# Gate and up products over both token streams at once in a four-layer transformer trunk

## Chip, cores and metric

The kernel runs as one launch on one core of a Trainium2 chip. The metric is the device time of that launch in microseconds (us); lower is better. The engines are named as in the profile: PE multiplies matrices, PEld is its load of the stationary operand, DVE, ACT and POOL are the vector, scalar and general engines, and SP issues the DMAs.

## What is computed

Two streams of 256 tokens by 1024 features pass through four layers: the latent tokens `x` (stream l) and the context tokens `ctx` (stream c). They share all weights. Each layer is

```python
h  = rmsnorm(x,   g[0]) * (1.0 + sc1)  + sh1
hc = rmsnorm(ctx, g[0]) * (1.0 + csc1) + csh1
y, yc = mixer(h, hc)          # layers 0 and 3: differential attention, 1: neighbourhood, 2: windowed
x = x + gt1 * rmsnorm(y, g[1])
h = rmsnorm(x, g[2]) * (1.0 + sc2) + sh2
x = x + gt2 * rmsnorm((silu(h @ w1) * (h @ w3)) @ w2, g[3])
# the same for ctx, but not after the attention of the last layer
```

Context tokens attend only to context tokens, latent tokens to both. The shifts, scales and gates come from `silu(c) @ ada_w[i] + ada_b[i]` (and from `c_ctx` for the context). The hidden width of the feed-forward part is 2816, which is 22 blocks of 128 columns for gate and 22 for up.

## The kernel before

**Arithmetic.** Every matrix product is done in three: each fp32 factor is split into a rounded part (hi) and the rest (lo), and `mm3` (L486 to L489) issues hi·hi, hi·lo and lo·hi into one sum. Weights come in units of 512 KB. `load_weight` (L494) loads a unit into `wr` by one DMA, ACT rounds it into `wh`, and DVE subtracts to get `wl` (L501). There are 3 tiles `wr`, and 5 each of `wh` and `wl` (RING), so at most five units are on the chip in split form.

**Products.** `feature_major` (L785) takes one unit of 128 columns of the weights for one stream: the weights are the stationary operand, h transposed is the moving one, 256 columns wide (the tokens of one stream). A unit is 8 blocks of features by 3 products, 24 matmuls, in two operations of 12. It serves q, k, gate and up. `token_major` (L794, for w2) and `block_unit_product` (L1119, for v and o) have the tokens as the stationary operand and the weights as the moving one, 512 columns wide. For gate and up, one PSUM bank per stream and pair holds gate in columns 0 to 255 and up in 256 to 511; then ACT takes the silu and DVE multiplies (L1270).

**Tiles of h.** h transposed lies in tiles of 128 features by 256 tokens: `hh` (hi) and `hl` (lo), 8 of each per stream, in four pools.

**Order.** Nothing runs in the order of the code. `Plan` collects operations with an engine, an estimated duration, a priority and their dependencies, schedules them four times over with a model of the engines, keeps the order of the schedule with the shortest modelled time, and emits each engine's instructions in that fixed order. The durations of PE in it are constants: 12 × 0.109 us for twelve matmuls of 256 columns, 6 × 0.216 us for six of 512; those of ACT and DVE come from `t_act` and `t_dve` (for n elements, `t_dve` gives 0.07 + 0.00104 × n us). The products of a stream keep their order (`chain`, L470). Stream l starts 21.5 us behind stream c in priority (LEAD), so that one stream's products run while the other one is in its norms.

**Beside it.** The shifts, scales and gates of the next layer are computed during gate and up: DVE multiplies and adds rows of `ada_w` (L605, L608), PE sums and transposes them (L615, L649), at a low priority.

**Stages.** By the lines that run, gate and up of layers 0, 1 and 2 lie at about 291 to 555, 933 to 1195 and 1515 to 1778 us from the start of the span, each followed by w2 for 120 us. Layer 3 has only stream l from its queries on; its gate and up run from 2093 to 2220 us.

Of the kernel before, what the change touches and what calls it, by code (L numbers as in the profile page):

```python
# [17 lines left out]
P = 128  # L18
# [38 lines left out]
X_LATE = False  # L57
LATE = 5
# [10 lines left out]
class Buf:  # L69
    """A piece of on-chip memory; `kind` names the slots that it may take, at the time when it is scheduled."""  # L70
# [8 lines left out]

class Bag(dict):  # L80
    """A set that keeps its order."""
# [21 lines left out]
class Plan:  # L103
    """Orders the operations of all engines: earliest first, then by priority, within the slots that there are."""
# [34 lines left out]
    def run(self):  # L139
        """Schedules again and again, each time by the latest starts that the schedule before would allow."""  # L140
# [178 lines left out]
def trunk(ctx: ExitStack, tc: tile.TileContext, a: dict, out: bass.AP, layers=tuple(range(DEPTH)), info=None):  # L319
# [47 lines left out]
    def tick(dt):  # L367
        clock[now[0]] += dt
# [8 lines left out]
    def act(o, i, func, dur, reads, writes, p=None, **kw):  # L377
        """o, i, and the bias/scale/accum_out in kw: functions that return the access, or constants."""
# [54 lines left out]
    def late_consts():  # L433
        """What the first attention needs."""
# [36 lines left out]
    def pe(dur, fn, reads, writes, p=None, also=(), unit=False):  # L471
# [4 lines left out]
        if unit:  # L476
            if now[0] in chain:
                o.after.add(chain[now[0]])
            chain[now[0]] = o
        anchor[now[0]] = o  # L480
        trail[now[0]].append(o)
        if p is None:
            tick(dur)
        return o
# [31 lines left out]
    def ada_load(raw, src, early=False):  # L516
        """Loads of these weights stay in order, and go no further ahead than the tiles and the stream allow."""
# [9 lines left out]
    def ada_first(i, r):  # L527
        """Shift and scale of 256 features, for the first layer: they come piece by piece."""
# [29 lines left out]
    def ada_groups(groups):  # L558
        """Yields after each slice of work; a group: layer, third, halves of it, parts (of 8) of the sum for the vector engine."""
# [5 lines left out]
    def spread(tag, i, m, what):  # L565
        """Vectors of both streams -> DRAM, for reading them on every partition. what: (name, column, function of (out, s))."""
# [24 lines left out]
    def ada_group(i, g, m, us, kd):  # L591
        """Columns g*2048 + u*1024 + j*256 + c stand in row 32j (latent) and 32j+1 (context), column u*256 + c."""
# [80 lines left out]

    def split(s, src_fn, src, hb, lb):
# [4 lines left out]
    def prenorm(s, i, which):  # L679
        """x -> h^T in parts, feature-major, one pair of buffers per 128 features."""  # L680
# [24 lines left out]
        for kp in range(4):  # L705
# [26 lines left out]
    def modulate_first(s, raw, r):  # L732
        """Two times 128 features of h^T in parts, for the first layer."""
# [6 lines left out]
        for kk in range(2):  # L740
            k = 2 * r + kk
            v, hb, lb = Buf("f1"), Buf("hh" + s), Buf("hl" + s)
# [7 lines left out]
    def on_all(s, i, nm):  # L750
        """A vector of 1024 features on every partition, in two halves."""
# [11 lines left out]
    def postnorm(s, i, which, y, final=False):  # L763
        """x += gate * rmsnorm(y): y is [token tile][half] in PSUM."""
# [20 lines left out]
    def feature_major(s, w, H, bank, c0, also=()):  # L785
        """bank[:, c0:c0+T] = (unit of weights)^T h^T."""
        wh, wl, h3, l3 = w
        for half in range(2):
# [3 lines left out]
            pe(12 * 0.109, go, [wh, wl] + [b for k in range(4 * half, 4 * half + 4) for b in H[k]], [bank], also=also, unit=True)  # L792

    def token_major(s, w, hb, lb, y, first, last):  # L794
        wh, wl, h3, l3 = w
        for t in range(2):
# [4 lines left out]
            pe(6 * 0.216, go, [wh, wl, hb, lb], [y[t][0], y[t][1]] if not first else [y[0][0], y[0][1], y[1][0], y[1][1]] if t == 0 else [y[t][0], y[t][1]], unit=True)  # L801

    def rope(bank):
        sw, t1 = Buf("f1"), Buf("f1")
        src = lambda: bank.ap[:, 0:T]
# [9 lines left out]
    def split_q(qs, buf, src):  # L815
        """Two heads of q^T * scale, each as parts stacked over the partitions."""
# [7 lines left out]
    def split_k(buf, src, place):  # L824
        """Two heads of k^T: per head parts (hi, lo), each on both halves of the partitions."""
# [36 lines left out]
    def flip(s, e, pt, qts):  # L862
        """e[q, keys] -> parts of its transpose in pt[pair of key tiles][keys, key tile, q]."""
# [18 lines left out]
    def pt_tiles(s, nkt):  # L882
        """P^T as parts (hi, lo) for each pair of key tiles: [keys, key tile, q]."""
# [5 lines left out]
    def att_a(S, s, j, L):  # L889
# [36 lines left out]
        pe(0.327 * nkt, pv, [b for q in pt for b in q] + [v[0] for v in vals], [(b, 0)])  # L926
# [11 lines left out]
    def att_bc(S, s, j, L):  # L938
# [11 lines left out]
        for m in range(2):  # L950
# [53 lines left out]
            pe(0.218 * nkt, go, [b for q in pt for b in q] + [v[0] for v in vals], [pv])  # L1004
# [7 lines left out]
    def bias_tile(h, qt):  # L1012
        """Relative-position bias and window of the neighbours; nothing is added for the context's keys, which come first."""
# [83 lines left out]
    def make_V(s, kind, y, half=0):  # L1097
        """The values as parts, token-major: V[t] -> access [tokens, head, (hi, lo), dims]."""
# [22 lines left out]
    def block_unit_product(s, w, H, y, h, pr):  # L1121
        """y[t][h] += tokens x (256 features) x (512 columns)."""
# [5 lines left out]
        for t in range(2):  # L1128
            def go(t=t):
# [4 lines left out]
            pe(6 * 0.216, go, [wh, wl] + [b[0::2] if isinstance(b, tuple) else b for kk in range(2) for b in H[2 * pr + kk]],  # L1134
               [y[0][h], y[1][h]] if pr == 0 and t == 0 else [y[t][h]], unit=True)

    def run_unit(s, L, unit, w):
# [4 lines left out]
        if nm == "v":  # L1142
# [3 lines left out]
            if kind == "C":  # L1146
# [4 lines left out]
                for t in range(2):  # L1151
# [7 lines left out]
                    pe(12 * 0.109, go, [wh, wl] + [b for kk in range(4) for b in H[4 * n + kk]], [S.y[t][0]], unit=True)  # L1159
# [12 lines left out]
        elif nm in "qk":  # L1172
            if nm == "q" and n == 0:
                S.o = Buf("oo" + s)
            b = Buf("bk" + s, cap=("proj" + s, CAP_P))
            place, also = None, []
            if nm == "q":
                also = [Buf("r2", cap=("qs", CAP_Q))]
            elif kind != "C":
                also = [Buf("r2", cap=("ks" + s, CAP_K[s])) for _ in range(2)]  # L1180
                place = lambda m: (also[m], lambda: also[m].ap)
            else:
                ra = S.ra

                def place(m):
                    c0 = 1024 + (2 * n + m) * 512
                    return ra, lambda: ra.ap[:, c0:c0 + 512].rearrange("p (l t) -> p l t", l=2)
            feature_major(s, w, S.H, b, 0, also)
            if s == "l" and kind != "B":
                buf, src = rope(b)  # L1190
            else:
                buf, src = b, lambda: b.ap[:, 0:T]
            if nm == "q":
                S.qs = also[0]
                split_q(S.qs, buf, src)
            elif kind == "C":
                for m, kt in enumerate(split_k(buf, src, place)):
                    S.KS[2 * n + m] = kt
            else:
                S.ks = split_k(buf, src, place)  # L1200
                if s == "c":
                    ctx_keys[n] = S.ks
            if (nm == "k" or kind == "C" and nm == "q") and not (kind == "C" and nm == "k") and not (last and s == "c"):
                boost[0] = BOOST[kind]
                (att_a if kind == "A" else att_bc)(S, s, n, L)
                boost[0] = 0.0
                if n == KD - 1:
                    S.gate = trail[s][-GATE[kind]]
        elif nm == "o":
# [7 lines left out]
            if h == 0:  # L1217
                for k in (2 * pr, 2 * pr + 1):
# [5 lines left out]
                    else:  # L1224
                        hb, lb = Buf("hh" + s), Buf("hl" + s)
# [15 lines left out]
        elif nm == "w2":  # L1241
# [3 lines left out]
            hb, lb = Buf("hh" + s), Buf("hl" + s)  # L1245
# [182 lines left out]
```

## Time and profile before

| | |
|---|---|
| device time, median of 3 runs | 2291.74 us |
| lowest and highest | 2291.06 and 2293.13 us |
| span of the profiled execution | 2287.6 us |
| median above that span | 4.1 us |
| PE busy | 2234.2 us, 98% of the span |
| PEld busy | 2064.8 us, 90% |
| DVE busy | 1646.0 us, 72% |
| ACT busy | 1072.1 us, 47% |
| granted clock of TensorE, mean | 0.997 |

The span goes from the first to the last instruction of the profiled execution. Its own total beside the span is not listed, so the 4.1 us are the distance of the median to that span. Matmuls overlap in the pipeline, so the busy time of PE does not tell how densely they are issued; the distance of their starts does.

### The profile page before, as it was taken

Reading aid. Unit: us, or ns where it says so; the run is one execution under the profiler, and the core shown is the slowest. Engines: PE = TensorE matmul, PEld = TensorE weight load, DVE = VectorE, ACT = ScalarE, POOL = GpSimd, SP = SyncE. Lnnn points to the kernel's source line nnn. Section 1 sums busy time; section 2 is a strip of 40 time slices with the busy share of each in tenths; the row PEclk is TensorE's granted clock in tenths of the full one; section 3 lists DMA queues with packets and bytes.
Section 4 is the critical chain, followed back from the end, with each engine's and each line's share of the span. In section 5 each row is a group of like instructions: output and inputs, shape, how many; then the busy total and the mean of one; then the engine's idle time right before and its main releaser. Section 6 shows DMA issues by size and latency. Waiting matters only on the chain.

```text
span 2287.6 us, 41639 instructions
## 1 busy us (share of the span) xinstructions
PE 2234.2 (98%) x16116; PEld 2064.8 (90%) x16116; DVE 1646.0 (72%) x3145; ACT 1072.1 (47%) x2305; POOL 219.7 (10%) x300
## 2 busy tenths in 40 slices
PE   7999999999999999999999999999999999998998
PEld 5899899999888998999998898899999888997997
DVE  5988699886354888978673389998777426896454
ACT  5478642223344776522233368852222325686443
POOL 0111100000010221100000033010000001320000
PEclk9999999999999999999999999999999999999999
DMA  9644366654233443665542330255555333444654
GB/s 305 207 124 125 93 225 204 217 191 150 86 130 98 111 101 107 195 197 185 189 157 92 129 93 20 75 166 189 192 181 176 102 111 111 125 116 145 184 188 139
DMA packets 369302, 339.30 MB, mean 148 GB/s; under 512 B 33120, under 2 KB 282960, under 8 KB 369104
## 3 DMA queue, kind: packets, MB, share of 16 engines
q1 hardware_dynamic: 369104, 336.63, 46.6%
q8 instruction: 127, 2.08, 0.4%
q14 instruction: 71, 0.58, 0.1%
HBM read 321.77 MB, written 1.17 MB: 141 GB/s over the span
## 4 chain that ended last, share of the span: by engine, by line
PE 84%; DVE 7%; ACT 4%; issue 2%; POOL 1%; DMA 1%; SPq 0%; DVEq 0%; ACTq 0%; POOLq 0%
PE bkl L487 14%; PE bkl L488 14%; PE bkl L489 14%; PE bkc L487 11%; PE bkc L489 11%; PE bkc L488 11%; ACT f L388 2%; DVE wl L501 1%; PE bkl L871 1%; PE bkc L615 1%; DVE col L859 1%; ACT r L388 1%; DVE r L879 1%; PE bkl L851 1%; PE bkl L713 1%
## 5 line engine op out<-in xcount | busy, mean ns | idle before, releaser
L501 DVE TENSOR_TENSOR wl<-wr,wh 128x1024 fp32r<-128x1024 f32 x380 | 473.3, 1247 | 380.5 <-ACT wh L388 379.3
L388 ACT ACTIVATE wh<-wr 128x1024 fp32r<-128x1024 f32 x380 | 402.3, 1060 | 697.6 <-PE bkl L488 379.8
L487 PE MATMUL bkl<-hhl,wh 128*128 128x256 f32 x1872 | 532.7, 285 | 0.0
L489 PE MATMUL bkl<-hhl,wl 128*128 128x256 f32 x1872 | 529.2, 283 | 0.0
L488 PE MATMUL bkl<-hll,wh 128*128 128x256 f32 x1872 | 528.4, 282 | 0.0
L487 PE MATMUL bkc<-hhc,wh 128*128 128x256 f32 x1456 | 413.6, 284 | 0.1
L489 PE MATMUL bkc<-hhc,wl 128*128 128x256 f32 x1456 | 411.2, 282 | 0.0
L488 PE MATMUL bkc<-hlc,wh 128*128 128x256 f32 x1456 | 410.9, 282 | 0.1
L608 DVE SCALAR_TENSOR_TENSOR f<-f,cs,f 128x512 f32<-128x512 f32 x556 | 384.7, 745 | 18.3 <-DMA f<-in_ada_w 18.2
L487 PEld LDWEIGHTS bkl<-hhl,wh 128*128 128x128 f32 x1872 | 357.3, 191 | 3.6 <-issue 3.3
L489 PEld LDWEIGHTS bkl<-hhl,wl 128*128 128x128 f32 x1872 | 357.6, 191 | 0.0
L488 PEld LDWEIGHTS bkl<-hll,wh 128*128 128x128 f32 x1872 | 357.4, 191 | 0.2
L487 PEld LDWEIGHTS bkc<-hhc,wh 128*128 128x128 f32 x1456 | 277.1, 190 | 3.5 <-issue 2.5
L488 PEld LDWEIGHTS bkc<-hlc,wh 128*128 128x128 f32 x1456 | 277.1, 190 | 0.8 <-DVE hlc L727 0.3
L489 PEld LDWEIGHTS bkc<-hhc,wl 128*128 128x128 f32 x1456 | 277.2, 190 | 0.0
L487 PE MATMUL bkl<-wh,hhl 128*128 128x512 f32 (+1 forms) x560 | 219.5, 392 | 0.0
L489 PE MATMUL bkl<-wh,hll 128*128 128x512 f32 (+1 forms) x560 | 217.0, 388 | 0.0
L488 PE MATMUL bkl<-wl,hhl 128*128 128x512 f32 (+1 forms) x560 | 217.0, 387 | 0.0
L487 PE MATMUL bkc<-wh,hhc 128*128 128x512 f32 (+1 forms) x472 | 186.3, 395 | 0.0
L488 PE MATMUL bkc<-wl,hhc 128*128 128x512 f32 (+1 forms) x472 | 183.0, 388 | 1.8 <-DVE wl L501 1.8
L489 PE MATMUL bkc<-wh,hlc 128*128 128x512 f32 (+1 forms) x472 | 183.0, 388 | 1.0 <-DVE hlc L677 1.0
L669 POOL TENSOR_SCALAR col<-col 128x1 f32<-128x1 f32 x58 | 37.0, 638 | 1505.0 <-ACT j L388 1459.4
(212 smaller groups left out, 3414.2 us busy)
## 6 DMA issues: line engine op xcount, KB each, us to landing
wr<-in_ffn_w SPq DMA_DIRECT2D x264, 512.0 KB, 3.7
f<-in_ada_w SPq DMA_DIRECT2D x384, 256.0 KB, 4.5
wr<-in_a_wqkv SPq DMA_DIRECT2D x48, 512.0 KB, 3.7
f<-gd SPq DMA_DIRECT2D x54, 256.0 KB, 4.9
r<-r SPq DMA_DIRECT2D x96, 128.0 KB, 2.6
wr<-in_b_wqkv SPq DMA_DIRECT2D x24, 512.0 KB, 3.7
wr<-in_a_wo SPq DMA_DIRECT2D x16, 512.0 KB, 3.7
wr<-in_c_wqkv SPq DMA_DIRECT2D x12, 512.0 KB, 3.7
```

The source lines that it names most:

```text
L388: nc.scalar.activation(o(), i(), func, **k)
L487: nc.tensor.matmul(o, lh, rh, start=first, stop=False)
L488: nc.tensor.matmul(o, lh, rl, start=False, stop=False)
L489: nc.tensor.matmul(o, ll, rh, start=False, stop=last)
L501: dve(lambda: nc.vector.tensor_tensor(l.ap, raw.ap, f32(h.ap[:]), ALU.subtract), t_dve(1024), [raw, h], [l], p)
L608: dve(lambda b=b, raw=raw, c=c: nc.vector.scalar_tensor_tensor(b.ap, raw.ap, c(), b.ap, ALU.mult, ALU.add), t_dve(512, extra=0.06), [raw, ...
L615: nc.tensor.matmul(acc.ap[32 * j:32 * j + 32, u * 256:(u + 1) * 256], lhs, tiles[j // 2].ap[:, (j % 2) * 256:(j % 2 + 1) * 256], start=fir ...
L669: op("pool", 0.25, lambda: nc.gpsimd.tensor_scalar(r.ap[:, 1:2], ss.ap[:, 0:1], ss.ap[:, 1:2], D * EPS, ALU.add, ALU.add), [ss], [r])
L713: nc.tensor.transpose(tp.ap[:, c0:c0 + P], xn[t, k // 4].ap[:, (k % 4) * P:(k % 4 + 1) * P], ident.ap)
L851: nc.tensor.matmul(o, q, kt()[:, 0, :], start=True, stop=False)
L859: dve(lambda: nc.vector.tensor_reduce(nm.ap[:, 0:n], b.ap[:].rearrange("p (i k) -> p i k", i=n), AX.X, ALU.max, negate=True), t_dve(512), ...
L871: nc.tensor.transpose(tp.ap[:, to * P:(to + 1) * P], e.ap[:, c * P:(c + 1) * P], ident.ap)
```

## The change

Gate and up of layers 0 to 2, from the third pair on (`ALONE = 2`), are done by one operation for both streams: the moving operand is h of context and latent side by side, 512 columns. For this, h lies in 8 tiles `both_h[k]` of shape 128 × (hi, lo) × (c, l) × 256. `View` hands out the part of such a tile as if it came from a pool, and `pair(s, k)` names the part of block k, so that a buffer now has a fixed place for each k where before any of 8 would do. Gate gets a whole bank and up another. One silu covers both streams, and two multiplications follow, one for each. The first two pairs, and all of layer 3, are done as before, stream by stream. The products of q and k go into a new function `head_unit`, which is called for one stream (`QK_BOTH` is False), with the same operations as before.

All constants for the durations of matmuls in the planner change, those of ACT, DVE, POOL and DMA do not.

```diff
+ALONE = 2
+QK_BOTH = False
...
-        pool("hh" + s, KD, ("hh" + s, (P, T), R32))
-        pool("hl" + s, KD, ("hl" + s, (P, T), R32))
...
+    both_h = []
+    for k in range(KD):
+        both_h.append(res.tile([P, 2, 2, T], R32, name=f"h{k}", tag=f"h{k}"))
+        for n, s in enumerate("cl"):
+            for m, x in enumerate("hl"):
+                pool(f"h{x}{s}{k}", 1, (f"h{x}{s}{k}", (P, T), R32), mem=View(both_h[k][:, m, n, :]))
...
+    def pe(dur, fn, reads, writes, p=None, also=(), unit=False, streams=None):
...
+        for s in streams or (now[0],):
+            if unit:
+                if s in chain:
+                    o.after.add(chain[s])
+                chain[s] = o
+            anchor[s] = o
+            trail[s].append(o)
+            if p is None:
+                clock[s] += dur
...
+    def pair(s, k):
+
+        return Buf(f"hh{s}{k}"), Buf(f"hl{s}{k}")
...
-            pe(12 * 0.109, go, [wh, wl] + [b for k in range(4 * half, 4 * half + 4) for b in H[k]], [bank], also=also, unit=True)
+            pe(12 * 0.120, go, [wh, wl] + [b for k in range(4 * half, 4 * half + 4) for b in H[k]], [bank], also=also, unit=True)
+
+    def feature_major_both(w, H, bank, also=()):
+
+        wh, wl, h3, l3 = w
+        for half in range(2):
+            def go(half=half):
+                for k in range(4 * half, 4 * half + 4):
+                    hi, lo = (both_h[k][:, m].rearrange("p s t -> p (s t)") for m in range(2))
+                    mm3(bank.ap[:], h3()[:, k, :], l3()[:, k, :], hi, lo, k == 0, k == KD - 1)
+            reads = [wh, wl] + [b for h in H for k in range(4 * half, 4 * half + 4) for b in h[k]]
+            pe(12 * 0.227, go, reads, [bank], also=also, unit=True, streams="cl")
...
-        pe(0.436, go, [qs] + [k[0] for k in keys], [b], also=[e])
+        pe(0.472, go, [qs] + [k[0] for k in keys], [b], also=[e])
...
-        pe(0.327 * nkt, pv, [b for q in pt for b in q] + [v[0] for v in vals], [(b, 0)])
+        pe(0.36 * nkt, pv, [b for q in pt for b in q] + [v[0] for v in vals], [(b, 0)])
...
-            pe(0.218 * nkt, go, [b for q in pt for b in q] + [v[0] for v in vals], [pv])
+            pe(0.24 * nkt, go, [b for q in pt for b in q] + [v[0] for v in vals], [pv])
...
+    def ffn_unit(unit, w):
+
+        nm, n = unit[0], unit[1]
+        bank = Buf("bkl", cap=("gu2", 4))
+        feature_major_both(w, [st[s].H for s in "cl"], bank)
+        if nm == "gate":
+            st["c"].gu2 = bank
+            return
+        gate_bank, sg = st["c"].gu2, Buf("f2")
+        boost[0] = BOOST["F"]
+        act(lambda: sg.ap, lambda: gate_bank.ap, AF.Silu, t_act(512), [gate_bank], [sg])
+        for i, s in enumerate("cl"):
+            g = st[s].g
+            dst, at = (g[0], n) if n < 16 else (g[1], n - 16)
+            dve(lambda i=i, dst=dst, at=at: nc.vector.tensor_tensor(
+                dst.ap[:, at, :], bank.ap[:, i * T:(i + 1) * T], sg.ap[:, i * T:(i + 1) * T], ALU.mult),
+                t_dve(T), [bank, sg], [(dst, at)])
+        boost[0] = 0.0
...
-            hb, lb = Buf("hh" + s), Buf("hl" + s)
+            hb, lb = pair(s, n % KD)
...
+            elif both and unit[0] in ("gate", "up") and unit[1] >= ALONE:
+                now[0] = "c"
+                ffn_unit(unit, w)
```

The six-matmul operations of w2, v and o likewise go from `6 * 0.216` to `6 * 0.227` in the planner, and those of v in layer 2 from `12 * 0.109` to `12 * 0.120`.

## Rows read from the trace of the kernel before

**Rows 1.** The page: share of engines, and the chain by engine.

```profile
PE 2234.2 (98%) x16116; PEld 2064.8 (90%) x16116; DVE 1646.0 (72%) x3145; ACT 1072.1 (47%) x2305; POOL 219.7 (10%) x300
...
PE 84%; DVE 7%; ACT 4%; issue 2%; POOL 1%; DMA 1%; SPq 0%; DVEq 0%; ACTq 0%; POOLq 0%
```

**Rows 2.** Busy time by stage: gate and up, and one w2.

```profile
core 0: us, PE busy (x) PEld busy (x) DVE busy (x) ACT busy (x) POOL busy (x), PEclk, DMA share, GB/s
291.00:555.00 264.00, 263.17 (x2254) 258.84 (x2253) 226.81 (x364) 75.12 (x125) 5.24 (x8) 1.00 0.62 204
555.00:675.00 120.00, 120.00 (x532) 98.73 (x531) 48.09 (x81) 40.55 (x74) 6.22 (x8) 1.00 0.31 106
933.00:1195.00 262.00, 262.00 (x2239) 258.66 (x2238) 208.43 (x330) 75.57 (x127) 5.28 (x8) 1.00 0.58 189
1515.00:1778.00 263.00, 262.05 (x2237) 258.41 (x2236) 207.03 (x337) 75.76 (x127) 6.23 (x8) 1.00 0.57 186
```

**Rows 3.** Forty-microsecond windows of PE alone: gate and up, then w2.

```profile
960.00:1000.00 40.00, 40.00 (x337) 1.00 0.64 205
...
1200.00:1240.00 40.00, 40.00 (x177) 1.00 0.28 97
```

**Rows 4.** Timeline of PE in w2: start, duration, shape.

```profile
559.70 0.40 PE L489 MATMUL bkc<-wh,hlc 128*128 128x512 f32 x1
...
561.10 0.39 PE L489 MATMUL bkc<-wh,hlc 128*128 128x512 f32 x1
561.33 0.39 PE L487 MATMUL bkl<-wh,hhl 128*128 128x512 f32 x1
...
563.37 0.39 PE L487 MATMUL bkl<-wh,hhl 128*128 128x512 f32 x1
```

**Rows 5.** Timeline of PE where stream l comes into gate, layers 0, 1, 2.

```profile
304.20 0.36 PE L487 MATMUL bkl<-hhl,wh 128*128 128x256 f32 x1
...
943.48 1.07 PE L713 MATMUL bkl<-ident,f 128*128 128x128 f32 x8
...
947.68 0.60 PE L713 MATMUL bkl<-ident,f 128*128 128x128 f32 x4
948.04 0.36 PE L487 MATMUL bkl<-hhl,wh 128*128 128x256 f32 x1
...
1528.23 0.36 PE L487 MATMUL bkl<-hhl,wh 128*128 128x256 f32 x1
```

**Rows 6.** Timeline of all engines from up to w2, layer 0.

```profile
552.50 0.28 PE L487 MATMUL bkc<-hhc,wh 128*128 128x256 f32 x1
...
552.98 1.33 ACT L388 ACTIVATE hhl<-gal 128x256 fp32r<-128x256 f32 x4
...
553.46 1.42 DVE L677 TENSOR_TENSOR hll<-gal,hhl 128x256 fp32r<-128x256 f32 x4
...
555.68 0.48 PE L487 MATMUL bkl<-wh,hhl 128*128 128x512 f32 x1
```

**Rows 7.** Groups of DVE and of ACT: count, busy, mean ns, idle before.

```profile
L501 DVE TENSOR_TENSOR wl<-wr,wh 128x1024 fp32r<-128x1024 f32 x380 | 473.3, 1247 | 380.5 <-ACT wh L388 379.3
...
L388 ACT ACTIVATE f<-bkl 128x256 f32<-128x256 f32 x104 | 38.3, 369 | 8.4 <-PE bkl L489 8.2
L388 ACT ACTIVATE f<-bkl 128x512 f32<-128x512 f32 x4 | 2.3, 596 | 0.5 <-PE bkl L713 0.5
```

**Rows 8.** Who waited for whom: in total, times, longest.

```profile
ACT wh L388 <- PE bkl L488: 379.8, 153, 5.2
```

**Rows 9.** Busy time by stage, the four stages of attention and their norms.

```profile
60.00:291.00 231.00, 228.43 (x1682) 203.68 (x1681) 192.80 (x405) 155.54 (x390) 35.82 (x40) 1.00 0.45 137
675.00:933.00 258.00, 255.16 (x1783) 236.22 (x1782) 199.47 (x440) 168.15 (x421) 53.11 (x80) 1.00 0.40 107
1315.00:1515.00 200.00, 189.97 (x1398) 177.31 (x1395) 182.04 (x527) 157.13 (x441) 47.38 (x68) 1.00 0.23 71
1897.00:2103.00 206.00, 192.23 (x1302) 177.04 (x1301) 164.90 (x318) 136.57 (x296) 43.55 (x48) 0.98 0.41 120
```

More of the change, by code (lines that the diff above doesn't have):

```diff
@@ L77, in __init__, with tile @@
             self.slot = -1
+class View:
+    def __init__(self, ap):
+        self.ap = ap
+    def tile(self, *args, **kwargs):
+        return self.ap
 class Bag(dict):
@@ L722, in prenorm @@
                 k = 2 * kp + kk
-                hb, lb = Buf("hh" + s), Buf("hl" + s)
+                hb, lb = pair(s, k)
                 src = lambda kk=kk, tp=tp: tp.ap[:, kk * T:(kk + 1) * T]
@@ L741, in modulate_first @@
             k = 2 * r + kk
[L742 removed]
+            v, (hb, lb) = Buf("f1"), pair(s, k)
             dve(lambda k=k, kk=kk, v=v: nc.vector.tensor_scalar(
@@ L800, in go, with rope @@
                     mm3(y[t][h].ap, lh, ll, h3()[:, h, :], l3()[:, h, :], first, last)
-            pe(6 * 0.216, go, [wh, wl, hb, lb], [y[t][0], y[t][1]] if not first else [y[0][0], y[0][1], y[1][0], y[1][1]] if t == 0 else [y[t][0], y[t][1]], unit=True)
-    def rope(bank):
+            pe(6 * 0.227, go, [wh, wl, hb, lb], [y[t][0], y[t][1]] if not first else [y[0][0], y[0][1], y[1][0], y[1][1]] if t == 0 else [y[t][0], y[t][1]], unit=True)
+    def rope(bank, c0):
         sw, t1 = Buf("f1"), Buf("f1")
-        src = lambda: bank.ap[:, 0:T]
+        src = lambda: bank.ap[:, c0:c0 + T]
         dve(lambda: nc.vector.stream_shuffle(sw.ap, src(), SWAP16), t_dve(T), [bank], [sw])
@@ L1133, in go, with head_unit, place_c @@
                         h3()[:, kk, :], l3()[:, kk, :], k == 0, k == KD - 1)
-            pe(6 * 0.216, go, [wh, wl] + [b[0::2] if isinstance(b, tuple) else b for kk in range(2) for b in H[2 * pr + kk]],
+            pe(6 * 0.227, go, [wh, wl] + [b[0::2] if isinstance(b, tuple) else b for kk in range(2) for b in H[2 * pr + kk]],
                [y[0][h], y[1][h]] if pr == 0 and t == 0 else [y[t][h]], unit=True)
+    def head_unit(streams, L, unit, w):
+        nm, n = unit[0], unit[1]
+        kind = MIXERS[L]
+        also, place = {}, {}
+        for s in streams:
+            S = st[s]
+            if nm == "q" and n == 0:
+                S.o = Buf("oo" + s)
+            if nm == "q":
+                also[s] = [Buf("r2", cap=("qs", CAP_Q))]
+            elif kind != "C":
+                also[s] = [Buf("r2", cap=("ks" + s, CAP_K[s])) for _ in range(2)]
+                place[s] = lambda m, bs=also[s]: (bs[m], lambda: bs[m].ap)
+            else:
+                also[s] = []
+                def place_c(m, ra=S.ra):
+                    c0 = 1024 + (2 * n + m) * 512
+                    return ra, lambda: ra.ap[:, c0:c0 + 512].rearrange("p (l t) -> p l t", l=2)
+                place[s] = place_c
+        b = Buf("bk" + streams[-1], cap=("proj" + streams[-1], CAP_P))
+        if len(streams) == 2:
+            feature_major_both(w, [st[s].H for s in streams], b, [x for s in streams for x in also[s]])
+        else:
+            feature_major(streams[0], w, st[streams[0]].H, b, 0, also[streams[0]])
+        for i, s in enumerate(streams):
+            now[0] = s
+            S = st[s]
+            if s == "l" and kind != "B":
+                buf, src = rope(b, i * T)
+            else:
+                buf, src = b, lambda c0=i * T: b.ap[:, c0:c0 + T]
+            if nm == "q":
+                S.qs = also[s][0]
+                split_q(S.qs, buf, src)
+            elif kind == "C":
+                for m, kt in enumerate(split_k(buf, src, place[s])):
+                    S.KS[2 * n + m] = kt
+            else:
+                S.ks = split_k(buf, src, place[s])
+                if s == "c":
+                    ctx_keys[n] = S.ks
+        for s in streams:
+            now[0] = s
+            S = st[s]
+            if (nm == "k" or kind == "C" and nm == "q") and not (kind == "C" and nm == "k") and not (L == DEPTH - 1 and s == "c"):
+                boost[0] = BOOST[kind]
+                (att_a if kind == "A" else att_bc)(S, s, n, L)
+                boost[0] = 0.0
+                if n == KD - 1:
+                    S.gate = trail[s][-GATE[kind]]
@@ new lines, in ffn_unit @@
+    def ffn_unit(unit, w):
+        nm, n = unit[0], unit[1]
+        bank = Buf("bkl", cap=("gu2", 4))
[12 more added lines that the diff above has]
+                t_dve(T), [bank, sg], [(dst, at)])
+        boost[0] = 0.0
@@ L1158, in run_unit @@
                     H, S_y = S.H, S.y
-                    pe(12 * 0.109, go, [wh, wl] + [b for kk in range(4) for b in H[4 * n + kk]], [S.y[t][0]], unit=True)
+                    pe(12 * 0.120, go, [wh, wl] + [b for kk in range(4) for b in H[4 * n + kk]], [S.y[t][0]], unit=True)
                 if n == 1:
@@ L1172, in run_unit @@
         elif nm in "qk":
[L1173 to L1208, printed above, removed]
+            head_unit((s,), L, unit, w)
         elif nm == "o":
@@ L1345, in trunk @@
             x_loads = None
-            for s in "cl" if both else "l":
-                now[0] = s
-                run_unit(s, L, unit, w)
+            if both and unit[0] in "qk" and QK_BOTH:
+                now[0] = "c"
+                head_unit("cl", L, unit, w)
+            elif both and unit[0] in ("gate", "up") and unit[1] >= ALONE:
+                now[0] = "c"
+                ffn_unit(unit, w)
+            else:
+                for s in "cl" if both else "l":
+                    now[0] = s
+                    run_unit(s, L, unit, w)
     plan.run()
```

12 lines of the change are left out of this document (1 added, 11 removed).

## The prediction

> **What bounds the kernel now.** I read the page first. PE is busy for 98% of the span and carries 84% of the chain that ended last [rows 1]. A busy PE may still be a PE that waits inside its pipeline, so the second view is the busy time by stage. In gate and up of layers 0 to 2 PE is idle for 0.8, 0 and 1.0 us of about 263 us each; PEld, the load of the stationary operand, is busy for 98% too; DVE stands at 86% in layer 0 and 79% in the other two, ACT at 29%; the granted clock is 1.00, the 2.4 GHz level [rows 2]. The third view, windows in which PE does nothing but one shape, tells how densely matmuls start, which their durations (0.28 and 0.39 us, overlapped) don't. An instruction is counted when it touches the window, so the distance of starts is (window + one duration) / count: (40 + 0.28) / 337 = 119.5 ns for 256 columns and (40 + 0.39) / 177 = 228.2 ns for 512 [rows 3, 4]. The reader is to see that twice the columns don't cost twice the time: two matmuls of 256 take 239.0 ns, one of 512 takes 228.2 ns. About 10.8 ns of each matmul is a price per instruction, and gate and up run at that pace without a hole. Nor are the weights late: the longest wait in total on ACT is the rounding of the next unit waiting for PE to give a place back [rows 8].
>
> **The change, part by part.**
>
> *The wide matmuls.* From the third pair on there are 20 pairs, so 40 units, in each of three layers: 120 units of 24 matmuls, 2,880 instructions of 512 columns in place of 5,760 of 256. The stationary operand is the same 128 × 128 block as before, loaded half as often. No row shows this operation itself: w2 has the length of the moving operand, the old gate has the stationary operand. I take the pace of w2, 228.2 ns: 2,880 × 10.8 ns = 31.1 us less. The bounds come from w2's own timeline: it has stretches at (563.37 − 561.33) / 9 = 226.7 ns, which gives 2,880 × 12.3 = 35.4 us, and at (561.10 − 559.70) / 6 = 233.3 ns, which gives 2,880 × 5.7 = 16.4 us [rows 4]. The middle of the three is the mean over 40 us, so it is the nearest. The slow end matters because gate and up move 205 GB/s beside the products and w2 97 [rows 3].
>
> A rule says less. The Trainium skill ("TensorE: Matmul & The Clock Gate", section "Back-to-back issue gap") gives the isolated distance of matmuls at the full clock as columns / 2.4 plus 2.5 ns, so a wide one would save only 2.5 ns, and 2,880 of them 7.2 us by an estimate from that page. The rows show 119.5 and 228.2 ns where the rule has 109.2 and 215.8, so the trace doesn't agree with it here, and the rows decide.
>
> *Stream l comes in.* Streams can no longer drift against each other from pair 3 on. Stream c has four units alone, 96 × 119.5 ns = 11.5 us, to cover the end of stream l's norm. In layers 0 and 2 stream l's first product stood at 304.20 and 1528.23, that is 13.2 us after the stage began at 291 and 1515 [rows 2, 5]. Two blocks of eight transposes of l, 1.07 us each, stand in that time, so c filled at most 11.1 us of it: covered, cost 0. In layer 1 it stood at 948.04, 15.0 us after 933; less one block of eight at 1.07 and two of four at 0.60 us that is 12.7 us, so c is up to 1.2 us short. But the first half of l's unit needs only the eight transposes at 943.48, and the last four, at 947.68, come just ahead of l's product because they were placed there. Between 0 and 1.2 us; I take 1 us.
>
> *From up to w2.* Before, l's products ended 24 matmuls ahead of c's: in layer 0 c still had from 552.50 on, and under that ACT and DVE split four blocks of l for w2 in 1.33 and 1.42 us; c ended at about 552.50 + 24 × 0.12 = 555.4 and w2 began at 555.68 [rows 6]. Now both streams end together. What replaces the cover is the second half of the last up, 12 × 228.2 ns = 2.7 us, since blocks 0 to 3 of h are free after the first half. The first product of w2 needs one block, 0.33 us on ACT and 0.36 us on DVE with the hops between the engines: hidden. If a weight subtraction of 1.25 us [rows 7] stands in front on DVE and the four blocks of both streams queue up, about 1.5 us shows. Between 0 and 1.5 us for each layer; I take 0.5 us, so 1.5 us in all.
>
> *ACT, DVE, PSUM, weights.* One silu of 512 columns for two of 256: 596 ns where 2 × 369 = 738 ns stood [rows 7], on an engine that is 29% busy: nothing either way. The multiplications stay. Gate now has a bank of its own, so its silu can run under up; two pairs still hold four banks. DVE's work in layer 0, 227 us, must fit into 264 − 10 = 254 us: 89%, still below PE. Five units of ring are five times 24 × 228.2 ns, 27 us of lead. A fixed place for each block of h binds nothing new, because the blocks were freed and taken in order of k before as well. All of this is hidden by PE's dense stream; without it, see the rivals.
>
> *The planner's constants.* Those of PE rise by 8 to 10% for matmuls of 256 columns and by 5% for 512. They do not change an instruction, only the fixed orders of all engines, above all in attention, where PE is idle 2.6 + 2.8 + 10.0 + 13.8 = 29.2 us of 895 [rows 9]. The new values agree with the rows (120 for 119.5, 227 for 228.2). But DVE's stay short: the planner has 0.07 + 0.00104 × 1024 = 1.135 us for the weight subtraction that took 1.247 [rows 7]. Before, 109 ns for 119.5 was short by the same 9%, so the proportion was right; now it isn't. A gain up to part of the 29 us is as possible as a loss; I take 0, with 5 us either way.
>
> **Sum.** 2287.6 − 31.1 + 1.0 + 1.5 = 2259.0 us of span. The median stands 4.1 us above the profiled span, and nothing in that part changes: 2291.7 − 28.6 = 2263.1 us. A difference under 0.2% (4.6 us) is about what the measurement can't tell from none.
>
> **The rivals.**
>
> 1. *The wide form saves little.* The price per instruction may belong to the narrow form's load of the operand and not come back: by the planner's old durations, 2 × 109 − 216 = 2 ns are saved for each wide matmul, 5.8 us, and 2291.7 − 5.8 + 2.5 = 2288.4 us, no change. The page's rule named above is of this kind. For it speaks that no row shows this very form; against it that w2's matmuls load a stationary block of the same size each time and still start 228.2 ns apart. Chance 0.05.
>
> 2. *The new order is worse in attention* (the other side). With PE's constants raised alone, the planner believes that softmax chains on DVE and ACT finish earlier against PE than they do, and puts products in front of results that aren't there yet. Place: the four attention stages, worst in layer 2, where DVE is busy for 182 of 200 us [rows 9]. Price: DVE and ACT are taken for 9% shorter than they are; 9% of DVE's 739 us there is 67 us of which PE would see what no other product covers. If half shows, 33 us, the time is 2263.1 + 33 = 2296 us: slower. It decides from 28.6 us of new idle time on. Against it: even with the old order PE lost only 29.2 us there, and the other stream's products fill in. Chance 0.07, 0.03 of it over 2296.3 us and the rest around no change or a smaller gain.
>
> 3. *DVE becomes the bound in layer 0.* 89% is a mean; if the sums for the next layer bunch so that a unit's subtraction comes later than the 27 us of lead allow, layer 0 keeps its length and loses its third of the gain, 10.4 us: 2273.5 us. Against it the long waits of ACT for a place [rows 8]. Chance 0.07.
>
> 4. *The handovers cost more.* With both streams bound together, PE stands idle at each end of the stage, 2 us at the first and 1.5 us at the second in each layer, 10.5 us in place of 2.5: 2271 us. Chance 0.15.
>
> **How the numbers follow.** Forecast 0.66 and the rivals 0.05, 0.07, 0.07 and 0.15. The predicted time is the likeliest, 2263.1 us. Its own bounds are 2263.1 − 4.3 (fast pace) − 5 (order) = 2254 and, for the slow pace, 2263.1 + 14.7 = 2278 us; rivals 3 and 4 lie inside. I give 2254 to 2278 us. Outside are rivals 1 and 2, 0.12, and some 0.05 of larger effects of order. Faster by over 0.2% are the forecast, rivals 3 and 4 and a part of rival 2: 0.90. Within 0.2%: rival 1 and a part of rival 2, 0.06. Slower: 0.04.
>
> **What the profile after would show.** The wide product right: some 2,880 matmuls of 512 columns with `h` as the moving operand, PE with about 13,200 instructions in place of 16,116, windows of 40 us in gate with about 177 counted; a count near 172 means the slow pace, near 185 would be more than any row here promises. Each stage shorter by 10 us. Stream l's entry right: idle time ahead of the first wide product under 2 us. The end right: w2 begins within 1 us of the last up. The order right: PE idle in the four attention stages between 24 and 34 us. The prediction is wrong if the wide matmuls start over 233 ns apart, if PE waits for `wl` in layer 0, or if attention loses more than 10 us against before.

## The result, and the profile after

The changed kernel takes 2343.86 us (median of 4 runs, 2341.35 to 2351.33) against 2291.4 us for the kernel before, a ratio of 1.023 (95% interval 1.0212 to 1.0248): 52 us slower where 29 us less was forecast. The span grew from 2287.6 to 2341.8 us.

The page of the changed kernel, shares of engines and the chain by engine:

```profile
span 2341.8 us, 35840 instructions
PE 2249.4 (96%) x13236; PEld 1933.5 (83%) x13236; DVE 1644.0 (70%) x3145; ACT 1063.8 (45%) x2245; POOL 214.9 (9%) x300
...
PE 77%; DVE 10%; ACT 6%; DMA 3%; issue 2%; POOL 1%; SPq 0%; DVEq 0%; ACTq 0%; POOLq 0%
```

The change did what it says: 2,880 matmuls fewer, exactly 16,116 − 13,236. But PE carries 77% of the chain in place of 84%, and DVE, ACT and DMA take up the 7 points that it lost [rows 1].

Windows of 40 us with one shape alone; two in gate and up, then w2 of layer 2 and of layer 3 (start and end of the window, its length, PE busy and count, clock, DMA):

```profile
1040.00:1080.00 40.00, 40.00 (x174) 1.00 0.61 200
1640.00:1680.00 40.00, 40.00 (x175) 1.00 0.59 192
1840.00:1880.00 40.00, 40.00 (x174) 1.00 0.26 92
2280.00:2320.00 40.00, 40.00 (x173) 1.00 0.56 195
```

(40 + 0.39) / 174 = 232.1 ns. The wide product runs at the slow pace of the prediction's bounds. The reader is to see the other two rows as well: w2 had 177 in such a window [rows 3] and has 174 and 173 now, and no instruction of w2 was changed, in layer 3 least of all.

Busy time by stage, with the columns of [rows 2, 9]: attention of the four layers, and 55 us at the end of attention of layer 1 that have no counterpart before:

```profile
60.00:303.00 243.00, 231.11 (x1663) 205.47 (x1662) 189.56 (x397) 155.12 (x385) 34.79 (x40) 0.98 0.41 126
...
687.00:945.00 258.00, 243.34 (x1685) 224.36 (x1684) 186.68 (x417) 155.71 (x392) 52.28 (x78) 0.99 0.38 102
945.00:1000.00 55.00, 48.82 (x306) 44.67 (x307) 44.95 (x84) 27.42 (x60) 7.60 (x11) 0.88 0.37 119
...
1352.00:1555.00 203.00, 192.49 (x1386) 176.89 (x1385) 176.49 (x520) 158.11 (x440) 46.03 (x68) 1.00 0.22 68
...
1940.00:2147.00 207.00, 188.41 (x1225) 170.68 (x1224) 157.09 (x311) 130.25 (x289) 42.53 (x48) 0.96 0.40 116
```

PE is idle for 11.9 + 14.7 + 10.5 + 18.6 = 55.7 us in the four attention stages, where it was 29.2 us [rows 9]; the prediction had named 24 to 34. And the granted clock, 1.00 in three of them before, is below it in three, 0.88 in the 55 us. What happens there is in the timeline of PE (in brackets the idle time before an instruction and what ended it):

```profile
943.73 0.66 PE L904 MATMUL bkl<-ident,f 128*128 128x128 f32 x4 [3.11 <-DVE f L1023]
945.00 0.33 PE L735 MATMUL bkc<-ident,f 128*128 128x128 f32 x1 [0.62 <-DVE f L722]
947.33 1.76 PE L735 MATMUL bkc<-ident,f 128*128 128x128 f32 x7 [2.00 <-DVE f L722]
950.66 2.79 PE L904 MATMUL bkl<-ident,f 128*128 128x128 f32 x12 [1.57 <-DVE f L1023]
...
953.46 0.41 PE L1035 MATMUL bkl<-r,vac 128*128 128x256 f32 x1
953.67 0.41 PE L1034 MATMUL bkl<-r,vac 128*128 128x256 f32 x1
...
956.50 0.28 PE L1035 MATMUL bkl<-r,val 128*128 128x256 f32 x1
956.62 0.28 PE L1034 MATMUL bkl<-r,val 128*128 128x256 f32 x1
```

PE has spent stream c's products with wo (the last starts at 937.85) and now waits for probabilities of stream l (L1023) and for stream c's norm (L722), with nothing left to put between. After that idle time the granted clock stands at its 1.2 GHz level for about 10 us (a window of PE: start and end, length, busy time and count, clock, DMA):

```profile
946.00:956.00 10.00, 7.10 (x32) 0.50 0.20 67
```

256 columns start 0.21 us apart at 953.46 and 0.12 us at 956.50. In the kernel before, the products with wo of both streams lay over these waits, and PE waited for nothing between 880 and 950 us; stream l's products with wo (L489 here) ran right up to the transposes of stream c's norm:

```profile
928.68 0.39 PE L489 MATMUL bkl<-wh,hll 128*128 128x512 f32 x1
928.91 1.03 PE L713 MATMUL bkc<-ident,f 128*128 128x128 f32 x8
```

In the changed kernel stream l then comes late into gate:

```profile
983.83 0.28 PE L507 MATMUL bkc<-h,wl 128*128 128x256 f32 x1
983.95 0.27 PE L735 MATMUL bkl<-ident,f 128*128 128x128 f32 x1
986.05 2.84 PE L735 MATMUL bkl<-ident,f 128*128 128x128 f32 x15 [1.83 <-DVE f L722]
988.54 0.56 PE L505 MATMUL bkl<-h,wh 128*128 128x256 f32 x1
```

Its transposes begin 39 us after stream c's (983.95 against 945.00) where it was 14.6 us before (943.48 [rows 5] against 928.91).

By layer, from the first transposes of stream c's norms (L713, later L735), in us of the span:

| | layer 0 | layer 1 | layer 2 | layer 3 | span |
|---|---|---|---|---|---|
| before | 675.2 | 639.5 | 583.0 | 389.9 | 2287.6 |
| after | 686.8 | 665.8 | 587.8 | 401.4 | 2341.8 |

Layer 1 lost most, 26.3 us. Layer 3 does nothing wide and still lost 11.5 us, so the loss is not in the wide products alone.

### The profile page after: what moved, and what is told of

The parts are those of the page before. It is cut to its first block, busy times and chain, and to the rows that moved or that the text cites. A ratio compares the mean times of both kernels' runs of the same rounds, so it can differ in the third digit from the quotient of the medians.

```text
span 2341.8 us, 35840 instructions
## 1 busy us (share of the span) xinstructions
PE 2249.4 (96%) x13236; PEld 1933.5 (83%) x13236; DVE 1644.0 (70%) x3145; ACT 1063.8 (45%) x2245; POOL 214.9 (9%) x300
## 4 chain that ended last, share of the span: by engine, by line
PE 77%; DVE 10%; ACT 6%; DMA 3%; issue 2%; POOL 1%; SPq 0%; DVEq 0%; ACTq 0%; POOLq 0%
PE bkl L505 18%; PE bkl L507 18%; PE bkl L506 18%; PE bkc L505 6%; PE bkc L507 6%; PE bkc L506 5%; ACT f L405 3%; ACT r L405 2%; DVE wl L519 2%; DMA r<-r 2%; DVE col L892 1%; PE bkl L904 1%; PE bkc L633 1%; DVE r L912 1%; DMA f<-in_ada_w 1%
## 5 line engine op out<-in xcount | busy, mean ns | idle before, releaser
L505 PE MATMUL bkl<-h,wh 128*128 128x256 f32 (+1 forms) x1872 | 642.2, 343 | 0.2 <-DVE f L840 0.2
L506 PE MATMUL bkl<-h,wh 128*128 128x256 f32 (+1 forms) x1872 | 636.8, 340 | 0.0
L507 PE MATMUL bkl<-h,wl 128*128 128x256 f32 (+1 forms) x1872 | 636.1, 340 | 0.0
L505 PEld LDWEIGHTS bkl<-h,wh 128*128 128x128 f32 x1872 | 354.2, 189 | 45.9 <-issue 2.5
L507 PEld LDWEIGHTS bkl<-h,wl 128*128 128x128 f32 x1872 | 354.0, 189 | 42.2
L506 PEld LDWEIGHTS bkl<-h,wh 128*128 128x128 f32 x1872 | 354.2, 189 | 41.1
L505 PE MATMUL bkl<-wh,h 128*128 128x512 f32 (+1 forms) x560 | 222.5, 397 | 0.9 <-ACT h L405 0.8
L507 PE MATMUL bkl<-wh,h 128*128 128x512 f32 (+1 forms) x560 | 219.3, 392 | 0.2 <-DVE h L1300 0.2
L506 PE MATMUL bkl<-wl,h 128*128 128x512 f32 (+1 forms) x560 | 219.0, 391 | 0.0
L505 PE MATMUL bkc<-wh,h 128*128 128x512 f32 (+1 forms) x472 | 187.1, 396 | 0.4 <-DVE ool L1040 0.4
L506 PE MATMUL bkc<-wl,h 128*128 128x512 f32 (+1 forms) x472 | 184.3, 391 | 1.1 <-DVE wl L519 1.1
L507 PE MATMUL bkc<-wh,h 128*128 128x512 f32 (+1 forms) x472 | 184.5, 391 | 1.0 <-DVE h L699 0.7
L506 PE MATMUL bkc<-h,wh 128*128 128x256 f32 x496 | 141.7, 286 | 6.9 <-DVE h L749 6.9
L505 PE MATMUL bkc<-h,wh 128*128 128x256 f32 x496 | 143.5, 289 | 0.4 <-DVE r L912 0.4
L505 PEld LDWEIGHTS bkl<-wh,h 128*128 128x128 f32 x560 | 105.4, 188 | 26.5 <-ACT h L405 2.6
L507 PEld LDWEIGHTS bkl<-wh,h 128*128 128x128 f32 x560 | 105.4, 188 | 25.1 <-DVE h L1300 0.6
```

The source lines that it names most:

```text
L505: nc.tensor.matmul(o, lh, rh, start=first, stop=False)
L506: nc.tensor.matmul(o, lh, rl, start=False, stop=False)
L507: nc.tensor.matmul(o, ll, rh, start=False, stop=last)
```

## The experiments

Three theories stood against each other. A: the planner's raised constants spoil the fixed orders, because PE's now stand in another proportion to those of ACT and DVE. B: binding both streams in one operation spoils them. C: any disturbance gives another order, by chance. Beside them stands the place of h in memory as the cause of the slower 512-column matmuls. Each ratio is against the kernel before, timed beside the run on the same chip; its medians there lay between 2292.7 and 2294.3 us. A planner constant changes no instruction, only the order in which each engine issues them and the buffers that they take.

**Constants and change taken apart.** The changed kernel with the old constants:

```diff
-            pe(12 * 0.120, go, [wh, wl] + [b for k in range(4 * half, 4 * half + 4) for b in H[k]], [bank], also=also, unit=True)
+            pe(12 * 0.109, go, [wh, wl] + [b for k in range(4 * half, 4 * half + 4) for b in H[k]], [bank], also=also, unit=True)
...
-            pe(12 * 0.227, go, reads, [bank], also=also, unit=True, streams="cl")
+            pe(12 * 0.216, go, reads, [bank], also=also, unit=True, streams="cl")
```

and so on for the rest.

> The changed kernel with the planner's old matmul durations (0.109 for 256 columns, 0.216 for 512, also for the wide product). Theory A (the raised constants alone spoil the fixed orders: attention of the four layers lost 39 us and the handover in layer 1 some 25 us): both come back, about 2285 us. Theory B (binding both streams in one operation spoils the orders, the constants matter little): it stays at 2330 us or more. Theory C (any disturbance of the planner gives another order, good or bad by chance): anywhere between, with the losses at other places than in the changed kernel.

Measured: 2301.12 us, ratio 1.0044 (1.003 to 1.0059): 43 us less than the changed kernel, but 16 us more than theory A gave. The lag of stream l in layer 1 is back at 14.6 us:

```profile
933.64 1.04 PE L735 MATMUL bkc<-ident,f 128*128 128x128 f32 x8
...
948.20 1.03 PE L735 MATMUL bkl<-ident,f 128*128 128x128 f32 x5
```

The pages of the two profiles show where most of the 43 us lie. PE is idle for 2299.0 − 2233.1 = 65.9 us here and for 2341.8 − 2249.4 = 92.4 us in the changed kernel, 26.5 us more; and the mean granted clock is 0.993 here and 0.988 there, which is another 0.005 × 2340 = 12 us at most, by an estimate from these numbers. The reverse, the kernel before with the new constants alone (the lines of the diff above that only change a number):

> The kernel before with nothing but the new matmul durations in the planner. Theory A: attention loses most of its 39 us, about 2325 us. Theory B: within 5 us of 2291. Theory C: anywhere from 2280 to 2330 us.

Measured: 2355.75 us, ratio 1.0275 (1.026 to 1.029): 63 us from constants alone, with the same instructions in another order. Attention of layers 1 and 3 in that run:

```profile
692.00:955.00 263.00, 245.86 (x1680) 228.07 (x1678) 184.97 (x406) 153.97 (x391) 50.81 (x78) 0.96 0.38 100
...
1955.00:2157.00 202.00, 183.96 (x1209) 167.11 (x1206) 154.03 (x305) 127.89 (x282) 42.46 (x48) 0.97 0.40 117
```

PE is idle 17.1 and 18.0 us (2.8 and 13.8 before [rows 9]), the clock falls again, and stream l lags 38.8 us in layer 1. It is not the pace of the matmuls: those of w2, v and o start 230.1 ns apart for 229.0 before, the 256-column products with weights 119.1 for 119.3, which nearly cancel. Theory B is out as the main cause: this kernel binds nothing.

**Only the new place of h.**

```diff
-ALONE = 2
+ALONE = 22
```

with the old constants.

> The changed kernel with no pair done wide and with the old constants: only the new place of h is left, 8 tiles with both streams and parts in one. If that place slows the 512-column matmuls of w2 (228 ns apart before, 232 after), w2 keeps 172 to 173 starts in 40 us and the time is about 2291 + 3144 x 3.5 ns = 2302 us. If the place does nothing, w2 shows 175 starts and the time is 2291 us, the orders being those of before.

Measured: 2296.49 us, ratio 1.0016 (1.0007 to 1.0025). Windows in gate (256 columns) and in w2:

```profile
960.00:1000.00 40.00, 40.00 (x340) 1.00 0.60 191
1220.00:1260.00 40.00, 40.00 (x173) 1.00 0.25 88
```

w2 has the slow pace, (40 + 0.39) / 173 = 233.5 ns, without any wide product, and the order of instructions on PE, ACT, DVE and POOL is that of the kernel before. The expectation missed that the 256-column matmuls would gain: 340 counted for 337 [rows 3], 118.5 ns. So most of the loss is given back.

**Theory A by proportion, from both sides.** The changed kernel with ACT and DVE raised as well; the kernel before with them shortened; the kernel before with the new constants and both raised:

```diff
-    return 0.07 + (0.00052 if fast else 0.00104) * n + extra
+    return 1.1 * (0.07 + (0.00052 if fast else 0.00104) * n + extra)
```

and likewise in `t_act` (0.91 in place of 1.1 where shortened).

> The changed kernel with the planner's durations of ACT and DVE raised by 10% too, so that their proportion to those of PE is as before. Theory A in its form that the proportion counts: attention comes back to within 10 us of before, about 2290 us. If only the size of PE's constants counts or the order is a matter of chance, no such return: 2310 to 2350 us.

> The kernel before with its own matmul constants and the planner's durations of ACT and DVE multiplied by 0.91: the same proportion as in the changed kernel, reached from the other side. Theory A by proportion: the same kind of loss as with the new matmul constants alone (2356 us), 2325 us or more, with most of it in attention and in the handover of layer 1. If the size of PE's constants is what counts: 2291 us within 8.

> The kernel before with the new matmul constants and ACT and DVE raised by 10% in the planner, nothing wide. Theory A by proportion: the 64 us that the new constants alone cost come back, 2291 to 2305 us. If only the size of PE's constants counts, or chance: about 2340 us.

Measured: 2304.54 us, ratio 1.0049 (1.0032 to 1.0066); 2335.22 us, 1.019 (1.0172 to 1.0209); 2313.82 us, 1.009 (1.0075 to 1.0105). Shortening the others does harm of the same kind as raising PE's, 41 us, with stream l 37.5 us behind in layer 1. Raising both together takes back 39 of the 43 us that the constants cost in the changed kernel (2304.54 us, with the old ones 2301.12) and 42 of the 63 us in the kernel before. So the proportion is the main cause. It doesn't explain all: 3 and 20 us stay. The durations of POOL, of the DMAs and of a hop between engines were not raised with the rest; whether that is the reason was not tested.

**Which constants.** On the kernel before, projections alone (12 × 0.120), attention products alone (0.472, 0.36, 0.24), and w2, v and o alone (6 × 0.227):

> The kernel before with only the constant of the 256-column projections raised (12 x 0.120: q, k, gate, up and v of layer 2); all together cost 64 us on this kernel. These matmuls are two thirds of PE's time in attention, so by proportion two thirds of the loss, 2330 us. If the attention products decide: 2300 us or less.

> The kernel before with only the constants of scores and of probabilities times values raised (0.472, 0.36, 0.24). By proportion a third of the loss or less, about 2305 us. If the attention products decide: 2340 us.

> The kernel before with only the constant of the six-matmul products of 512 columns raised (6 x 0.227: w2, v, o). If the losses add up, the rest of the 64 us, 34 us: 2328 us. If the loss comes from several constants being off the proportion together: 2291 to 2305 us.

Measured: 2317.44 us, ratio 1.0102 (1.0087 to 1.0117); 2300.99 us, 1.0031 (1.002 to 1.0042); 2319.27 us, 1.0117 (1.01 to 1.0134). That is 23, 7 and 26 us more, together 56 of 63: they nearly add up, and no single constant is the culprit. The split was not as expected: by shares of PE's time in attention the projections should have cost some 38 us and w2, v and o less than they.

**The place of the operands.** The compiled program gives the address of every tile, and the distance of each matmul's start to the next can be set against it. Of 512-column matmuls on end that have the remainders named:

| kernel | remainder of the addresses by 256: moving, stationary | distances | mean ns |
|---|---|---|---|
| before | 0, 0 | 1908 | 227.6 |
| place of h alone | 0, 128 | 2079 | 232.8 |
| old constants, wide product | 128, 0 | 2212 | 232.7 |

The test puts `wh`, `wl` and h, in this order, behind 128 bytes of padding:

```diff
+    pad = res.tile([P, 32], F32, name="pad", tag="pad")
+    for x in ("wh", "wl"):
+        own = {f"{x}{i}": res.tile([P, 1024], R32, name=f"{x}{i}", tag=f"{x}{i}") for i in range(RING)}
+        pool(x, RING, (x, (P, 1024), R32), mem=Fixed(own))
```

(`Fixed` hands out the tile of the given tag.) Once on the wide kernel with old constants, once on the kernel before:

> The wide product with the planner's old constants, and the tiles wh, wl and h placed at multiples of 256 bytes (in the changed kernel h lies 128 bytes off). Theory of the place: in the kernel before, matmuls of 512 columns start 226.7 ns apart where both operands lie at multiples of 256 bytes and 230 to 233 where one doesn't; all 5,776 of them then start about 227 apart in place of 232.4, which is 5,776 x 5.5 ns = 32 us less than the 2301 us of the run with old constants, some 4 us given back by the 256-column ones: about 2273 us. If the place is not the cause: 232 ns and 2300 us again.

> The kernel before with nothing changed but the place of wh, wl and the tiles of h, at multiples of 256 bytes. Theory of the place: w2, v and o, 3,000 matmuls of 512 columns, go from 229.0 to 227 ns, 7 us less: about 2285 us; the 256-column ones go from 119.3 to 119.6 ns, 3 us back at most. If the place is not the cause: 2291 us and 229 ns.

Measured: 2279.15 us, ratio 0.9936 (0.992 to 0.9953), all 512-column matmuls at 227 ns, 22 us less than with h in the other place (expected were 28). Windows in gate and in w2:

```profile
1040.00:1080.00 40.00, 40.00 (x178) 1.00 0.63 205
1220.00:1260.00 40.00, 40.00 (x178) 1.00 0.27 92
```

And 2294.62 us, ratio 1.0003 (0.9994 to 1.0013): there w2, v and o gained (229.0 to 227.4 ns), but the 9,820 matmuls of 256 columns went from 119.3 to 119.9 ns and took it back, so the 2285 us expected did not come. In both pairs (old constants with and without padding, the kernel before with and without it) the traces show the same order of instructions on PE, ACT, DVE and POOL, so the place is all that differs. The traffic of the DMAs is not the cause: gate has the fast pace here at 205 GB/s, and w2 had the slow one at 88 GB/s in the run with the place of h alone.

**The handover.** In the wide kernel with old constants and two pairs alone, stream c's first products in gate wait for their own h (timeline of PE, layer 0):

```profile
293.96 0.39 PE L506 MATMUL bkc<-h,wh 128*128 128x256 f32 x1 [0.86 <-DVE h L749]
296.07 0.39 PE L506 MATMUL bkc<-h,wh 128*128 128x256 f32 x1 [1.49 <-DVE h L749]
```

On the version of 2279 us, `ALONE = 3` and then `ALONE = 4`:

> The wide product with old constants and operands at multiples of 256 bytes (2279 us), the first three pairs stream by stream instead of two. Each layer gives 48 wide matmuls back, 48 x 12.9 ns = 0.6 us, 1.9 us in all. If the stalls at the handovers (idle time of gate, up and w2 is 10 to 13 us a layer there, 6 to 8 in the kernel before) come from stream c having too little to do alone, 3 us a layer come back: about 2272 us. If they don't: 2281 us.

> The 2270 us version with four pairs done stream by stream. If three pairs already cover the handover: 48 more wide matmuls a layer are given back, 1.9 us in all, 2272 us. If stream c is still short of work: another 3 us or more a layer, 2262 us.

Measured: 2270.38 us, ratio 0.9899 (0.9882 to 0.9915), and 2272.13 us, 0.9908 (0.9894 to 0.9923). With three pairs those waits are gone: what is left between 286 and 310 us is one of 0.9 us for stream l's norm. In the version of 2279 us PE waits 2.4, 2.4 and 2.1 us at the start of gate in the three layers, 6.9 us in all, and for nothing between up and w2; so most of the 8.8 us is seen in these waits and the rest was not traced. The fourth pair only gives wide matmuls back.

**Best version.** Three pairs, padding, old constants: 2270.38 us, 21 us under the recorded time of the kernel before, and so faster than both kernels of this document. Its 40 us windows in gate (the first two) and w2:

```profile
960.00:1000.00 40.00, 40.00 (x195) 1.00 0.68 217
1020.00:1060.00 40.00, 40.00 (x178) 1.00 0.61 199
1200.00:1240.00 40.00, 40.00 (x178) 1.00 0.26 85
```

The second and third have the same pace, (40 + 0.39) / 178 = 226.9 ns; the first still holds narrow matmuls. Three more runs on it or on its forerunner. ACT and DVE 10% longer, on the version of 2279 us:

> The same 2279 us kernel with the old matmul constants, and ACT and DVE 10% longer in the planner: the proportion moved to the other side of the kernel before. If only a planner that thinks too well of ACT and DVE does harm, no loss, or up to 10 us less: 2270 to 2280 us. If any departure from the proportion for which the other settings were found does harm: 2300 us or more.

All constants of the change in the best version:

> The 2270 us version with all the matmul constants of the change. If the constants are the main cause of the loss: 2315 to 2335 us, attention and the handover of layer 1 losing as in the changed kernel. If they only hurt along with the place of the operands or the short handover: 2275 us.

The best version without the padding:

> The 2270 us version without the 128 bytes of padding, so wh, wl and h all lie 128 bytes off a multiple of 256, in the same order and with the same order of instructions. If the distance to a multiple of 256 counts: starts 230 to 232 ns apart in place of 227, some 5,600 x 3.5 ns = 20 us, 2290 us. If only the distance between the two operands counts: 227 ns and 2270 us.

Measured: 2286.09 us, ratio 0.9968 (0.9957 to 0.9978), 7 us worse than without, which neither expectation gave: a planner that thinks worse of ACT and DVE loses too, but far less than one that thinks too well of them. Then 2321.44 us, 1.0126 (1.0111 to 1.0142): the constants cost 51 us here as well. And 2271.97 us, 0.9908 (0.9893 to 0.9922), with these windows in gate and w2:

```profile
1020.00:1060.00 40.00, 40.00 (x178) 1.00 0.61 202
1200.00:1240.00 40.00, 40.00 (x178) 1.00 0.25 87
```

All operands lie 128 bytes off there, and the pace is 227 ns. The order of instructions is again the same. My theory that multiples of 256 matter falls; what counts is that moving and stationary operand have the same remainder. This is shown for stretches in which all operands agree. In the run with old constants one of the five slots of `wh` and `wl` lies at remainders 128 and 64, and the matmuls with that slot start 230 to 234 ns apart, also those whose own two operands both leave 128.

## Why the prediction was wrong

- **The planner's constants: the step that failed.** "I take 0, with 5 us either way." They cost 43 us here (2343.9 against 2301.1), 63 on the kernel before, 51 in the best version. The prediction had seen that PE's constants rise alone and that DVE's stay 9% short, and priced it as rival 2, at 33 us, with a chance of 0.07. The mechanism of rival 2 is the one the traces show: products stand in front of results that aren't there yet, and PE waits. What misled was to read PE's small idle time in attention as proof that much could not be lost there; it was small with an order made at the old proportion, and an order made at another has other waits. Rival 2 named the place wrongly: the worst was layer 1, not layer 2. Of the prediction's three signs of being wrong, this one came true: attention lost more than 10 us.
- **The wide matmuls: right mechanism, wrong size in this kernel.** Forecast 10.8 ns each, 31.1 us. By before's narrow pace it was 2 × 119.5 − 232.1 = 6.9 ns, 20 us. With operands of equal remainder it is 2 × 119.5 − 226.9 = 12.1 ns, 35 us, and rival 1 is refuted: the price per instruction does come back. The 2.5 ns per matmul of the Trainium skill ("TensorE: Matmul & The Clock Gate", section "Back-to-back issue gap") fit neither of these. The two paces that the prediction read as its bounds [rows 4] are two places as well: in the stretch at 226.7 ns both operands leave remainder 0, in the one at 233.3 ns two of three matmuls have a stationary `hhc` at 128. The prediction looked to the DMA traffic for the slow end.
- **What I had counted as untouched.** The new place of h slowed 3,096 matmuls of w2, v and o by 3.3 ns, 10 us; the narrow ones that are left gained some 0.5 ns each, 2 us. "A fixed place for each block of h binds nothing new" looked at waiting only, not at where the place is.
- **The handovers.** Forecast 2.5 us, rival 4 10.5 us; a third pair alone brought 8.8 us. The size is near rival 4's, but that is partly luck: all the waits seen stand at the start of gate and none between up and w2. The place was not mainly stream l's entry, as argued, but stream c's own first products, put before their h was ready.
- **DVE as the bound in layer 0 (rival 3)** didn't show: PE waited for `wl` once in layer 0, 2.4 us in attention, and never in gate.
- **The sum.** Against before: −20 (wide), +10 and −2 (place), +43 (constants), +9 (handover) gives +40 of the 52 us. Some 9 us more are attention of layers 1 and 3 in the run with old constants, 258.2 and 195.8 us for 253.8 and 191.4, of which the place of h holds a small part; I found no single cause for them, and by theory C they may be chance of the order.

What stays open: why the planner's order is as sensitive as it is in layer 1. In the four runs that lose over 40 us to constants (the changed kernel, new constants alone, ACT and DVE shortened, best version with new constants) stream c's last product with wo starts 15 to 19 us ahead of stream l's last attention product; in the kernel before and with old constants it starts 5 to 7 us behind it. But it starts 16 us ahead also with ACT and DVE 10% longer, which lost only 7 us, and 1 us behind with the constants of w2, v and o alone, which lost 26; so this early end alone does not make the loss. Open too are the 3 and 20 us by which raising both sides together falls short, and the losses of 7 to 26 us in the other runs with changed constants, which proportion alone does not tell from a chance of the order.

## What to carry to other kernels

Constants of a planner that fixes the order of several engines are a set: a truer value for one engine alone can be worse than equally wrong ones for all, so change them together, and time the constants alone before anything rides on them. A wide matmul saves the price per instruction of the narrow pair, but look where a rearranged tile comes to lie: the pace of operations that the change never touched tells. When a gain fails to appear, split the change into its constants, its places and its operations first; here each had its own sign.

## What the runs showed of the hardware that was not expected

- Matmuls of 512 columns (fp32r) on end start 226.9 ns apart when all their operands' addresses leave the same remainder by 256, 0 (best version) or 128 (without the padding), and about 232.5 ns apart when one operand leaves 0 and the other 128 (place of h alone, old constants). For 256 columns it is the other way: 119.8 ns with equal remainders (best version), 118.5 ns with 0 and 128. Why is not settled by these runs.
- In the changed kernel PE is idle for 3.1, 0.6 and 2.0 us ahead of 943.7, 945.0 and 947.3 us, and the granted clock stands at the 1.2 GHz level from 946 to 956 us (0.88 over 945 to 1000 us). So such waits cost more than their length: 256 columns then start 0.21 us apart in place of 0.12.
